# A hybrid attention layer on one core: difference product six segments later, four heads' sums in one bank, x's rows turned on TensorE

## The chip, the cores and the metric

One Trainium2 chip, one of its cores. The metric is the device time of one execution in microseconds (us), shorter is better; of several runs the median is given.

## The reference, cut to what matters

One layer over x of 2048 positions and 1024 channels, float32. The rows are RMS-normed and projected once; three causal mixers read the projection, each result is multiplied by a SiLU gate, and one output projection is added to x.

```python
h = rms_norm(x, norm_g)
proj = h @ w_in
# A: 8 heads of 64, softmax attention
sc = rms(q) . rms(k) / 8 + c[t] - c[s],   c = cumsum(log_sigmoid(ff + b_f))
fox = softmax(sc, s <= t) @ v
# B: 4 groups of 64
pool = (window_mean(px, w) - px) @ w_pool * scale,   w = 2, 4, 8, 16
# C: 4 heads of 64, stick-breaking
a[t, s] = sigmoid(z[t, s]) * prod over s < j < t of (1 - sigmoid(z[t, j]))
sb = a @ v
out = x + concat(fox * silu(fg), pool * silu(pg), sb * silu(sg)) @ w_out
```

The stick-breaking weights are differences of running products, so the kernel multiplies the running products by differences of neighbouring rows of v. It gets those differences from a small matrix product: this is the "difference product".

## The kernel before, in words

**Precision.** A value that a matmul reads is split into two fp16 halves, high and low (`pairs16`, L338: the high half on ScalarE at L340, the low one on VectorE at L341), and three products are summed (L318).

**Stages.** The 2048 positions are 16 blocks of 128, taken from the last to the first (i counts them, j = 15 - i is the place). There are five projections: Fox heads 0 to 3 ("a"), Fox heads 4 to 7 ("b"), stick-breaking ("s"), pooling ("p"), output ("o"). `units` lists them: 16 of a, 16 of b, 16 of s with the 16 of p between them, 16 of o. `projections` is one long generator over the units; a unit yields after each *segment*, 3 matmuls of 128x512, and has 16 segments (pooling 8). Each segment calls `tick`, which counts down the waiting list of `later(k, fn)`: fn is issued k segments later. At the start of a unit `need_x` makes the next unit's x.

**x.** In stage a, `make_x` (L362) loads 128 rows (xn, L345, on SP's queue), sums their squares (ScalarE L351), and `transpose_rows` (L370) splits them into ppx (L340, L341), transposes ppx into xTx by one DMA from SP's queue (L374, 2048 columns), and parks xTx in DRAM two segments later from ScalarE's queue (L380). Stages b, s and p load it from there. xTx has two buffers. The first three units (blocks 15, 14 and 13) are prepared in `opening`; block 15 is used there in another form, so it is made once more for its parked copy alone.

**Attention.** `plan` lists 48 rows of blocks, each with four heads. For one head `qk` computes the scores of a block against all later places in the list (PSUM tile sp, L403, with a mask product L405), and makes weights: for Fox VectorE adds the forget term and finds the maximum (L735), ScalarE takes exp (L745); for stick-breaking ScalarE takes the sigmoid (L874), POOL masks the diagonal (L876) and VectorE scans the product (L882). `split_t` (L415) splits the weights into pp (ScalarE L429, VectorE L432) and transposes pp into tt by DMA from SP's queue (L434). Three heads later (`DEPTH`) `pv` sums weights times values into a PSUM tile o (L445, L446; stick-breaking L902 to L904). The dictionary `LEADS` fixes how many segments of projection lie between these steps.

**What the change touches.** In Fox, a head's sums stand as 128 columns (high and low half of v) in a bank of their own; VectorE adds the two halves into om (L779) after each head, and after the fourth POOL multiplies om by the reciprocal sums (L758). In stick-breaking, three matmuls of 64 columns sum into 64 columns, and four heads share one tile (L902 to L904). `steps` (L813), called at the end of a stick-breaking unit, forms the difference product pd (L820) from the values vr that were split just before (L340, L341), and splits it into Vs and vo. The PSUM tiles pqk, pvg, pf, pd, o, pr and pp (pooling) come from one pool of four banks (tag "pj"); the scores have the other four.

**Order.** Each engine runs its instructions in a fixed order. It is chosen when the program is built: by priority and by an estimate of when each can start, so instructions of different steps can stand among each other.

Of the kernel before, what the change touches and what calls it, by code (L numbers as in the profile page):

```python
# [30 lines left out]
LB = 4  # L31
SPD = 6
KPD = 2
MXD = 0
GTD = 0
BAL = 1
# [70 lines left out]
M3 = 2  # L107
M4 = 2
HOOK2 = 4
X1 = 1  # L110
X0 = 2
PBK = 4
# [12 lines left out]
def hybrid(ctx: ExitStack, tc, xN, w_in, w_pT, w_out, ng, b_f, qg, kg, w_pool, p_scale, bands, out):  # L125
# [19 lines left out]
    def pick(pattern, k):  # L145
        return {"v": v, "g": g, "s": s}[pattern[k % len(pattern)]]
# [36 lines left out]
    g.affine_select(tri, ones, [[-1, P]], ALU.is_ge, 0.0, base=0, channel_multiplier=1)  # L183
    id16 = const.tile([P, P], BF16, name="id16")
    g.tensor_copy(id16, ident)
    zero = at.tile([P, P], BF16, name="zero", tag="oa")
    g.memset(zero, 0.0)
    cmask = const.tile([P, P], BF16, name="cmask")
# [181 lines left out]
    def transpose_rows(src, scale, tag, park=None):  # L370
        pp = at.tile([P, 2 * D], F16, name=f"pp{tag}", tag="pp", bufs=PB)
        pairs16(pp[:, 0:D], pp[:, D:2 * D], src, scale[:, 0:1], pick(XLO, park or 0))
        x = xp.tile([P, 2, KT, P], F16, name=f"xT{tag}", tag="xT", bufs=XB)
        sy.dma_start_transpose(x.rearrange("p a k t -> p (a k) t"), pp)  # L374
        if park is not None:
            keep_x(park, x)
        return x

    def keep_x(j, x):
        later(KPD, lambda: dq(QPARK).dma_start(xTd[j], x))  # L380
# [53 lines left out]
            sy.dma_start_transpose(tt[:, :2 * n * G // P, :], pp[:, :2 * n * G])  # L434
        return tt[:, o_ // P:(o_ + 2 * n) // P]

    def pv(o, h, parts, Vc):
        first = True
        for n_, (c0, c1_, tt) in enumerate(parts):
            nb = (c1_ - c0) // P  # L440
            for b in range(nb):
                jj = c0 // P + b
                vt = Vc[jj // 4][:, jj % 4, h, :]
                last = n_ == len(parts) - 1 and b == nb - 1
                t.matmul(o[:, 0:P], tt[:, b, :], vt, start=first, stop=False)  # L445
                t.matmul(o[:, 0:HD], tt[:, nb + b, :], vt[:, 0:HD], start=False, stop=last)  # L446
                first = False

    def heads(ap):
        return ap.rearrange("p (h d) -> p h d", h=NH)  # L450
# [42 lines left out]
    class Fox:  # L493
# [256 lines left out]
        def weighted(self, i, sums):  # L750

            la, n_ = sums
            if n_ == 2:
                v.tensor_tensor(la[:, 0], la[:, 0], la[:, 1], ALU.add)
            rl = sm.tile([P, NH], F32, name=f"rl{self.ph}_{i}", tag="rl")
            v.reciprocal(rl, la[:, 0])
            v.tensor_scalar(rl, rl, self.iv[:, 0:1], None, ALU.mult, ALU.bypass)
            pick(OMS, 0).tensor_tensor(heads(self.om), heads(self.om), rl.unsqueeze(2).broadcast_to([P, NH, HD]), ALU.mult)  # L758

        def pv(self, i, h, parts, rl):  # L760
            j = NT - 1 - i
            if h == 0:
                self.om = at.tile([P, 256], F32, name=f"om{self.ph}_{i}", tag="om")
            self.finish(self.om, h, parts, f"{self.ph}_{i}_{h}")
            if h == NH - 1:
                self.weighted(i, rl)
                c = self.col
                om = self.om

                def send():  # L770
                    dq(QMIX).dma_start(mix[j][:, c:c + 256], om)
                    mixed.add((self.ph, j))

                later(MXD, send)

        def finish(self, om, h, parts, tag):
            o = po.tile([P, 512], F32, name=f"o{tag}", tag=ot)
            pv(o, h, parts, self.Vc)
            v.tensor_reduce(om[:, h * HD:(h + 1) * HD], o[:, 0:P].rearrange("p (a d) -> p d a", a=2), AX.X, ALU.add)  # L779

# [3 lines left out]
    class Stick(Fox):  # L786
# [54 lines left out]
        def proj(self, i, x):  # L841
            w = self.w
            j = NT - 1 - i
            pqk = pj.tile([P, 512], F32, name=f"pqks_{i}", tag="pj")
            if i in IS:
                pvg = pj.tile([P, 512], F32, name=f"pvgs_{i}", tag="pj")
                yield from together([project(pqk, x, w, 0, 0, 512), project(pvg, x, w, 0, 512, 512)])
            else:
                yield from project(pqk, x, w, 0, 0, 512)
            qT = stacks(f"s_{i}", j, pqk[:, 0:256], pqk[:, 256:512], 1.0 / WS, self.Kc)  # L850
            if i not in IS:
                pvg = pj.tile([P, 512], F32, name=f"pvgs_{i}", tag="pj")
                yield from project(pvg, x, w, 0, 512, 512)
            vt = at.tile([P, NH, P], F16, name=f"vr_{i}", tag="fq", bufs=2)
            pairs16(vt[:, :, 0:HD], vt[:, :, HD:P], heads(pvg[:, 0:256]), 1.0 / WS)
            self.vr[i] = vt
            keep_gate("s", i, j, pvg[:, 256:512], w.iw, 768)
            self.steps(i, j)
            self.ctx[i] = qT

        def qk(self, i, h):
# [27 lines left out]
        def pv(self, i, h, parts, left):  # L889

            j = NT - 1 - i
            if h == 0:
                self.o = po.tile([P, 512], F32, name=f"os_{i}", tag=ot)
            o = self.o[:, h * HD:(h + 1) * HD]
            first = True
            for n_, (c0, c1_, tt) in enumerate(parts):
                nb = (c1_ - c0) // P
                for b in range(nb):
                    jj = c0 // P + b
                    vt = self.own[i][:, h] if jj == j else self.Vc[jj // 4][:, jj % 4, h, :]  # L900
                    last = n_ == len(parts) - 1 and b == nb - 1
                    t.matmul(o, tt[:, b, :], vt[:, 0:HD], start=first, stop=False)  # L902
                    t.matmul(o, tt[:, b, :], vt[:, HD:P], start=False, stop=False)
                    t.matmul(o, tt[:, nb + b, :], vt[:, 0:HD], start=False, stop=last)  # L904
                    first = False
            if h == NH - 1:
                om = at.tile([P, 256], F32, name=f"oms_{i}", tag="om")
                g.tensor_tensor(heads(om), heads(self.last), left.unsqueeze(2).broadcast_to([P, NH, HD]), ALU.mult)
                v.scalar_tensor_tensor(om, self.o[:, 0:256], self.io[:, 0:1], om, ALU.mult, ALU.add)
                self.own.pop(i)  # L910
                c = self.col

                def send():
                    dq(QMIX).dma_start(mix[j][:, c:c + 256], om)
                    mixed.add((self.ph, j))

                later(MXD, send)

# [200 lines left out]
    def projections():  # L1119
        for u, (n, i) in enumerate(units):  # L1120
            need_x(u + (2 if units[u + 2:u + 3] == [(4, 0)] and OA else LAH[n]))
            if i == 0 and n:
                phases[n].start()
            gen = phases[n].proj(i, xs.pop(u, None))
            yield from with_tail(gen) if (n, i) == (4, 0) else gen
            if i == NT - 1 and n < 3:
                with first(HLW):
                    load_weights((1, 2, 4)[n])
            if n == 2 and i == 1:
                load_weights(3)  # L1130
# [181 lines left out]
```

## Time and profile before

| | |
|---|---|
| median of 3 runs | 1382.42 us (1378.74 to 1386.62) |
| the profiled execution: its own time | 1382.85 us |
| its span, first to last instruction | 1381.1 us |
| mean granted TensorE clock | 0.943 of 2.4 GHz |
| TensorE busy | 1185.5 us (86%) |
| VectorE busy | 1006.6 us (73%) |
| ScalarE busy | 751.6 us (54%) |
| POOL busy | 304.6 us (22%) |

PE is TensorE's matmuls, PEld its weight loads, DVE is VectorE, ACT ScalarE, POOL GpSimd, SP the engine whose queue issues most DMAs. Times in the trace are us from the start of the span. "<-" behind a row names what ended the idle time before it. A busy TensorE is not one at its peak: durations of neighbouring matmuls overlap, so the pitch is read from the distance of their starts.

### The profile page before, as it was taken

What the parts mean: (1) busy time and instruction counts of PE and PEld (TensorE: products, weight loads), DVE (VectorE), ACT (ScalarE), POOL (GpSimd) and SP (SyncE); (2) the same over time, 40 slices, a digit from 0 to 9 for tenths busy, and PEclk for the clock granted to TensorE, in tenths of its full rate; (3) what the DMA queues carried; (4) which work ended last, traced back from release to release, by engine and by line L of the source; (5) the groups of instructions that cost most, each with busy time, mean ns of one, the idle gap of its engine ahead of it and who ended that gap; (6) DMA issues with size and microseconds to landing.
All of it is one profiled execution on the core that took longest, in us unless ns stands there. A gap on an engine that the chain in (4) does not pass through costs nothing.

```text
span 1381.1 us, 24952 instructions
## 1 busy us (share of the span) xinstructions
PE 1185.5 (86%) x9068; PEld 634.9 (46%) x9068; DVE 1006.6 (73%) x2165; ACT 751.6 (54%) x1429; POOL 304.6 (22%) x471
## 2 busy tenths in 40 slices
PE   7786978787887798998978888988996998779998
PEld 3343534344444355554545444444553554444443
DVE  5677868887887568789888765767785788956541
ACT  6456657666666457677667744545554565421210
POOL 0121221211011222112112252433321214313300
PEclk9888999898998899999999999999998999989999
DMA  6659999999999999999999987886898889999763
GB/s 220 175 127 209 215 207 187 233 205 204 245 212 196 232 196 244 202 192 198 178 243 187 206 190 165 180 180 147 179 178 158 157 202 269 217 273 293 203 179 92
DMA packets 617067, 275.25 MB, mean 199 GB/s; under 512 B 552560, under 2 KB 590832, under 8 KB 616944
## 3 DMA queue, kind: packets, MB, share of 16 engines
q1 hardware_dynamic: 605600, 239.93, 82.0%
q10 hardware_dynamic: 10832, 33.67, 7.9%
q8 instruction: 71, 1.16, 0.4%
q14 instruction: 52, 0.43, 0.1%
q0 software_dynamic: 512, 0.07, 0.0%
HBM read 102.60 MB, written 34.67 MB: 99 GB/s over the span
## 4 chain that ended last, share of the span: by engine, by line
PE 47%; DMA 21%; DVE 11%; issue 9%; ACT 6%; SPq 3%; POOL 2%; ACTq 0%; POOLq 0%; DVEq 0%
PE pr L318 8%; DMA tta<-ppa 5%; DMA ttb<-ppb 5%; PE pqkb L318 4%; PE pvgb L318 4%; PE pqks L318 4%; DMA xTx<-ppx 3%; DVE rrs L882 3%; PE pqka L318 3%; PE pvgs L318 3%; PE pvga L318 3%; PE pp L318 3%; PE spb L403 2%; PE spa L403 2%; PE sps L403 2%
## 5 line engine op out<-in xcount | busy, mean ns | idle before, releaser
L318 PE MATMUL pr<-wo,xTm 128*128 128x512 f16 x768 | 171.0, 384 | 8.4 <-DMA xTm<-ppm 5.7
L429 ACT CAST pps<-rrs 128x640 f16<-128x640 f32 (+7 forms) x96 | 76.1, 795 | 122.1 <-DVE rrs L882 106.5
L882 DVE TENSOR_TENSOR_SCAN rrs<-rrs 128x640 f32<-128x640 f32 (+7 forms) x64 | 104.3, 1636 | 50.3 <-POOL rrs L876 42.3
L318 PEld LDWEIGHTS <-xTm 128*128 128x128 f16 x768 | 75.4, 99 | 100.3 <-DMA xTm<-ppm 6.8
L318 PEld LDWEIGHTS <-xTs 128*128 128x128 f16 x768 | 74.1, 99 | 92.3 <-issue 10.8
L318 PEld LDWEIGHTS <-xTb 128*128 128x128 f16 x768 | 74.5, 101 | 85.0 <-issue 10.8
L745 ACT ACTIVATE La<-La,nma 128x640 f32<-128x640 f32 (+7 forms) x96 | 85.3, 889 | 49.4 <-DVE nma L739 44.5
L745 ACT ACTIVATE Lb<-Lb,nmb 128x640 f32<-128x640 f32 (+7 forms) x96 | 85.5, 891 | 48.3 <-DVE nmb L739 48.1
L318 PEld LDWEIGHTS <-xTx 128*128 128x128 f16 x720 | 70.4, 102 | 84.4 <-issue 16.4
L432 DVE TENSOR_TENSOR pps<-rrs,pps 128x640 f16<-128x640 f32 (+7 forms) x96 | 93.5, 988 | 16.4 <-ACT pps L429 16.0
L318 PE MATMUL pp<-auxp,xTp 128*128 128x512 f16 x384 | 97.8, 407 | 0.0
L318 PE MATMUL pqkb<-wb,xTb 128*128 128x512 f16 x384 | 96.6, 399 | 0.0
L432 DVE TENSOR_TENSOR ppb<-Lb,ppb 128x640 f16<-128x640 f32 (+7 forms) x96 | 87.8, 927 | 11.3 <-ACT ppb L429 11.2
L445 PE MATMUL oa<-Va,tta 128*128 128x128 f16 x544 | 62.5, 228 | 37.2 <-DMA tta<-ppa 30.1
L432 DVE TENSOR_TENSOR ppa<-La,ppa 128x640 f16<-128x640 f32 (+7 forms) x96 | 89.8, 954 | 5.5 <-ACT ppa L429 5.4
L318 PE MATMUL pqks<-ws,xTs 128*128 128x512 f16 x384 | 93.2, 388 | 0.4 <-ACT ws L276 0.4
L318 PE MATMUL pvgb<-wb,xTb 128*128 128x512 f16 x384 | 93.4, 386 | 0.0
L318 PE MATMUL pvgs<-ws,xTs 128*128 128x512 f16 x384 | 90.5, 379 | 1.7 <-DVE ym L1004 1.7
L874 ACT ACTIVATE rrs<-sps,nc 128x640 f32<-128x640 f32 (+7 forms) x96 | 79.9, 862 | 21.1 <-PE sps L403 11.6
L403 PE MATMUL spa<-Ka,qTa 128*128 128x512 f16 (+3 forms) x320 | 78.2, 357 | 13.4 <-DVE mma L735 12.0
L318 PE MATMUL pqka<-wa,xTx 128*128 128x512 f16 x336 | 87.1, 406 | 0.0
L445 PE MATMUL ob<-Vb,ttb 128*128 128x128 f16 x544 | 61.4, 224 | 28.7 <-DMA ttb<-ppb 28.2
(306 smaller groups left out, 2788.0 us busy)
## 6 DMA issues: line engine op xcount, KB each, us to landing
xn<-in_xN_dram SPq DMA_DIRECT2D x16, 512.0 KB, 5.4
xTd<-xTx ACTq DMA_DIRECT2D x16, 512.0 KB, 4.5
xTb<-xTd ACTq DMA_DIRECT2D x16, 512.0 KB, 4.4
xTs<-xTd ACTq DMA_DIRECT2D x16, 512.0 KB, 4.5
xTp<-xTd ACTq DMA_DIRECT2D x16, 512.0 KB, 3.9
go<-gat SPq DMA_DIRECT2D x16, 512.0 KB, 7.0
mt<-mix SPq DMA_DIRECT2D x16, 512.0 KB, 5.5
xr<-in_xN_dram SPq DMA_DIRECT2D x16, 512.0 KB, 4.5
```

The costliest lines, as they stand in the source:

```text
L318: t.matmul(psum, x[:, xa, kt, :], wt[:, wa, c0:c0 + n], start=(kt == 0 and i == 0), stop=(kt == KT - 1 and i == 2))
L403: t.matmul(sp[:, b - c0 + off:e - c0 + off], qT[:, a * NH + h, :], Kc[b // 512][:, h, b % 512:b % 512 + e - b], start=(a == 0), stop=(a == ...
L429: s.copy(hi, p32)
L432: lo_eng.tensor_tensor(lo, p32, hi, ALU.subtract)
L445: t.matmul(o[:, 0:P], tt[:, b, :], vt, start=first, stop=False)
L745: s.activation(ls[a], ls[a], AF.Exp, bias=nm[:, 0:1], accum_out=la[:, a, h:h + 1])
L874: s.activation(gg, sp, AF.Sigmoid, scale=self.nc2[:, 0:1])
L882: v.tensor_tensor_scan(gg, gg, gg, init, ALU.mult, ALU.bypass)
```

## The change

Three edits and two constants. `steps` is called six segments after the end of its unit and not at once. Fox's sums take stick-breaking's form: one function `pv` for both, three matmuls of 64 columns for a block, four heads in one tile o; L779 goes, and the multiplication by the reciprocals reads o itself, on VectorE. In stage a, `transpose_rows` splits as before, but the turning is issued eleven segments later: 16 transposes of 128x128 on TensorE against an fp16 identity, in two PSUM tiles of tag "pj", each copied into xT by ScalarE; xT is allocated only then. The output stage's transposes, and the two made in the opening for blocks 14 and 13, stay DMAs.

```diff
+TURN = 11
+STL = 6
+    idh = const.tile([P, P], F16, name="idh")
+    g.tensor_copy(idh, ident)
...
     def transpose_rows(src, scale, tag, park=None):
         pp = at.tile([P, 2 * D], F16, name=f"pp{tag}", tag="pp", bufs=PB)
         pairs16(pp[:, 0:D], pp[:, D:2 * D], src, scale[:, 0:1], pick(XLO, park or 0))
-        x = xp.tile([P, 2, KT, P], F16, name=f"xT{tag}", tag="xT", bufs=XB)
-        sy.dma_start_transpose(x.rearrange("p a k t -> p (a k) t"), pp)
-        if park is not None:
+        if park is None:
+            x = xp.tile([P, 2, KT, P], F16, name=f"xT{tag}", tag="xT", bufs=XB)
+            sy.dma_start_transpose(x.rearrange("p a k t -> p (a k) t"), pp)
+            return x
+        made_x = []
+
+        def turn():
+            x = xp.tile([P, 2, KT, P], F16, name=f"xT{tag}", tag="xT", bufs=XB)
+            for a in range(2):
+                pt = pj.tile([P, 1024], F16, name=f"pt{tag}_{a}", tag="pj")
+                for b in range(KT):
+                    t.transpose(pt[:, b * P:(b + 1) * P], pp[:, a * D + b * P:a * D + (b + 1) * P], idh)
+                s.copy(x[:, a], pt.rearrange("p (k t) -> p k t", k=KT))
+            made_x.append(x)
             keep_x(park, x)
-        return x
+
+        later(TURN, turn)
+        return made_x
...
-    def pv(o, h, parts, Vc):
+    def pv(o, parts, vt):
...
-                vt = Vc[jj // 4][:, jj % 4, h, :]
-                t.matmul(o[:, 0:P], tt[:, b, :], vt, start=first, stop=False)
-                t.matmul(o[:, 0:HD], tt[:, nb + b, :], vt[:, 0:HD], start=False, stop=last)
+                vh = vt(c0 // P + b)
+                t.matmul(o, tt[:, b, :], vh[:, 0:HD], start=first, stop=False)
+                t.matmul(o, tt[:, b, :], vh[:, HD:P], start=False, stop=False)
+                t.matmul(o, tt[:, nb + b, :], vh[:, 0:HD], start=False, stop=last)
...
-            pick(OMS, 0).tensor_tensor(heads(self.om), heads(self.om), rl.unsqueeze(2).broadcast_to([P, NH, HD]), ALU.mult)
+            om = at.tile([P, 256], F32, name=f"om{self.ph}_{i}", tag="om")
+            v.tensor_tensor(heads(om), heads(self.o[:, 0:256]), rl.unsqueeze(2).broadcast_to([P, NH, HD]), ALU.mult)
+            return om
...
             if h == 0:
-                self.om = at.tile([P, 256], F32, name=f"om{self.ph}_{i}", tag="om")
-            self.finish(self.om, h, parts, f"{self.ph}_{i}_{h}")
+                self.o = po.tile([P, 512], F32, name=f"o{self.ph}_{i}", tag=ot)
+            pv(self.o[:, h * HD:(h + 1) * HD], parts, lambda jj: self.Vc[jj // 4][:, jj % 4, h, :])
...
-        def finish(self, om, h, parts, tag):
-            o = po.tile([P, 512], F32, name=f"o{tag}", tag=ot)
-            pv(o, h, parts, self.Vc)
-            v.tensor_reduce(om[:, h * HD:(h + 1) * HD], o[:, 0:P].rearrange("p (a d) -> p d a", a=2), AX.X, ALU.add)
...
-            self.steps(i, j)
+            later(STL, lambda: self.steps(i, j))
...
+            if i not in self.own:
+                tick(1 << 30)
...
-            gen = phases[n].proj(i, xs.pop(u, None))
+            x = xs.pop(u, None)
+            if isinstance(x, list):
+                if not x:
+                    tick(1 << 30)
+                x = x[0]
+            gen = phases[n].proj(i, x)
```

A call `tick(1 << 30)` issues everything that still waits in the list at once.

## Rows read from the trace of the kernel before

**Rows 1.** The page: busy us of each engine, share of the span, instructions.
```profile
PE 1185.5 (86%) x9068; PEld 634.9 (46%) x9068; DVE 1006.6 (73%) x2165; ACT 751.6 (54%) x1429; POOL 304.6 (22%) x471
```

**Rows 2.** Busy us by stage; columns: stretch, length, PE, PEld, DVE, ACT, POOL, clock, DMA.
```profile
43.50:365.00 321.50, 259.15 (x2003) 142.27 (x1999) 246.63 (x785) 194.93 (x452) 61.85 (x87) 0.91 0.97 201
365.00:700.00 335.00, 296.49 (x2265) 163.25 (x2265) 263.47 (x654) 219.65 (x456) 59.75 (x83) 0.95 1.00 211
700.00:1150.00 450.00, 388.15 (x3336) 211.38 (x3337) 335.53 (x450) 252.12 (x408) 127.64 (x256) 0.95 0.86 182
```

**Rows 3.** TensorE's waits, 43.5 to 365 us; columns: total us, times, longest.
```profile
PE pf L327 <- DMA xTx<-ppx: 19.0, 6, 8.8
PE oa L445 <- DMA tta<-ppa: 17.6, 10, 6.3
...
PE pvga L318 <- DVE oma L779: 2.2, 1, 2.2
```

**Rows 4.** The chain that ended last, 43 to 365 us, by line (cut at its end).
```profile
by line: DMA tta<-ppa 15.0%; DMA xTx<-ppx 15.0%; PE pqka L318 14.8%; PE pvga L318 14.2%; PE spa L403 7.3%; issue 4.4%; PE oa L445 4.4%; DVE La L735 4.0%; DMA wrb<-in_w_in_dram 2.2%; DMA xTd<-xTx 2.2%; PE oa L446 2.0%; ACT La L745 1.3%; ACT 
```

**Rows 5.** TensorE's waits, 700 to 1150 us.
```profile
PE pd L820 <- ACT vr L340: 23.3, 6, 9.8
...
PE pd L820 <- DVE vr L341: 5.0, 2, 3.7
```

**Rows 6.** Timeline around the longest of these waits: start, length, instruction.
```profile
1063.37 0.37 PE L820 MATMUL pd<-vr,sel 128*128 128x256 f16 x1 [9.75 <-ACT vr L340]
1063.54 6.27 PE L318 MATMUL pp<-auxp,xTp 128*128 128x512 f16 x15
...
1061.99 1.04 ACT L429 CAST pps<-rrs 128x1024 f16<-128x1024 f32 x1 [6.16 <-DMA tts<-pps]
...
1074.52 2.16 DVE L882 TENSOR_TENSOR_SCAN rrs<-rrs 128x768 f32<-128x768 f32 x1 [2.15 <-POOL rrs L876]
```

**Rows 7.** Timeline of TensorE: four Fox pairs, from L446 to L446; 14 stick sums.
```profile
603.28 0.19 PE L446 MATMUL ob<-Vb,ttb 128*128 128x64 f16 x1
...
603.62 0.19 PE L446 MATMUL ob<-Vb,ttb 128*128 128x64 f16 x1
...
916.46 0.19 PE L903 MATMUL os<-Vs,tts 128*128 128x64 f16 x1
...
916.84 0.19 PE L904 MATMUL os<-Vs,tts 128*128 128x64 f16 x1
```

**Rows 8.** Groups of instructions: count, busy us, mean ns, idle us before them.
```profile
L779 DVE TENSOR_REDUCE oma<-oa 128x64 f32<-128x128 f32 x64 | 17.9, 282 | 25.2 <-PE oa L446 25.0
...
L779 DVE TENSOR_REDUCE omb<-ob 128x64 f32<-128x128 f32 x64 | 18.0, 283 | 19.2 <-PE ob L446 18.8 <-issue 0.3
...
L1004 DVE TENSOR_TENSOR ym<-po,auxp 128x256 f32<-128x256 f32 x16 | 6.6, 413 | 0.0
...
L758 POOL TENSOR_TENSOR omb<-omb,rlb 128x256 f32<-128x256 f32 x16 | 11.9, 744 | 70.0 <-issue 42.0 <-DVE nmb L739 21.1 <-DVE omb L779 6.6
```

**Rows 9.** Timeline: one row's first sum, and the last head's reduction.
```profile
253.66 0.22 PE L445 MATMUL oa<-Va,tta 128*128 128x128 f16 x1
...
281.89 0.29 DVE L779 TENSOR_REDUCE oma<-oa 128x64 f32<-128x128 f32 x1 [1.06 <-PE oa L446]
```

**Rows 10.** DMA issues: the transposes of x, median us from issue to landing.
```profile
xTx<-ppx SPq DMA_TRANSPOSE x16, 4.5
```

**Rows 11.** A group of ScalarE, 43.5 to 365 us: reading 128x512 out of PSUM.
```profile
L706 ACT ACTIVATE qna<-pqka 128x512 f32<-128x512 f32 x13 | 7.7, 589 | 8.7 <-PE pqka L318 8.3 <-DVE sta L341 0.4
```

**Rows 12.** Timeline: pvga's start and the next unit's split, first and last late one.
```profile
94.59 3.62 PE L318 MATMUL pvga<-wa,xTx 128*128 128x512 f16 x16
...
106.64 1.28 DVE L341 SCALAR_TENSOR_TENSOR ppx<-xn,r,ppx 128x1024 f16<-128x1024 f32 x1 [1.78 <-ACT ppx L340]
...
324.86 1.89 PE L318 MATMUL pvga<-wa,xTx 128*128 128x512 f16 x8
...
335.18 1.28 DVE L341 SCALAR_TENSOR_TENSOR ppx<-xn,r,ppx 128x1024 f16<-128x1024 f32 x1 [0.16 <-issue]
```

More of the change, by code (lines that the diff above doesn't have):

```diff
@@ L441, in pv @@
             for b in range(nb):
-                jj = c0 // P + b
-                vt = Vc[jj // 4][:, jj % 4, h, :]
+                vh = vt(c0 // P + b)
                 last = n_ == len(parts) - 1 and b == nb - 1
-                t.matmul(o[:, 0:P], tt[:, b, :], vt, start=first, stop=False)
-                t.matmul(o[:, 0:HD], tt[:, nb + b, :], vt[:, 0:HD], start=False, stop=last)
+                t.matmul(o, tt[:, b, :], vh[:, 0:HD], start=first, stop=False)
+                t.matmul(o, tt[:, b, :], vh[:, HD:P], start=False, stop=False)
+                t.matmul(o, tt[:, nb + b, :], vh[:, 0:HD], start=False, stop=last)
                 first = False
@@ L762, in pv @@
             if h == 0:
-                self.om = at.tile([P, 256], F32, name=f"om{self.ph}_{i}", tag="om")
-            self.finish(self.om, h, parts, f"{self.ph}_{i}_{h}")
+                self.o = po.tile([P, 512], F32, name=f"o{self.ph}_{i}", tag=ot)
+            pv(self.o[:, h * HD:(h + 1) * HD], parts, lambda jj: self.Vc[jj // 4][:, jj % 4, h, :])
             if h == NH - 1:
-                self.weighted(i, rl)
+                om = self.weighted(i, rl)
                 c = self.col
-                om = self.om
                 def send():
@@ L891, in pv @@
             j = NT - 1 - i
+            if i not in self.own:
+                tick(1 << 30)
             if h == 0:
                 self.o = po.tile([P, 512], F32, name=f"os_{i}", tag=ot)
[L894 to L905, printed above, removed]
+            pv(self.o[:, h * HD:(h + 1) * HD], parts, lambda jj: self.own[i][:, h] if jj == j else self.Vc[jj // 4][:, jj % 4, h, :])
             if h == NH - 1:
```

## The prediction

> **What bounds the kernel now.** I read the page first, for the whole span, then the busy time by stage, then the waits of TensorE stage by stage, and last the chain and single stretches of the timeline. TensorE is the busiest engine, 1185.5 us or 86% of the span [rows 1]. The stages differ, in the DMA too [rows 2]. From 43.5 to 365 us (first Fox group, where x is also made) TensorE is busy 259.2 of 321.5 us, so idle 62.3, at a mean granted clock of 0.91 (1 is 2.4 GHz, 0.5 is 1.2), with a DMA share of 0.97. The second Fox group (to 700) has 38.5 us of idle at a DMA share of 1.00; stick-breaking and pooling (to 1150) 61.9 us at 0.86. So time can come only from TensorE's idle stretches, and what fills them must not lengthen its work.
>
> What ended those stretches: in the first Fox stage x's transposed rows ended 19.0 us in 6 waits and the transposed probabilities 17.6 us in 10 [rows 3]. The chain says more than the idle time does: DMA of xTx holds 15.0% of the stage, some 48 us, as much as tta [rows 4]. In the stick stage the difference product (pd) waits for its own values: 23.3 us for ScalarE and 5.0 for VectorE, 28.3 in 8 waits [rows 5].
>
> **Part 1, the difference product six segments later.** Nothing is added or removed: at most six matmuls and two splits for each of 16 blocks move, no DMA moves, and they pass projection segments on TensorE and scans, casts and splits on ScalarE and VectorE. The longest wait shows what is behind them [rows 6]: the cast that ScalarE starts at 1061.99, just before vr, had waited 6.16 us for a DMA to free its buffer, and TensorE stands 9.75 us at the first pd with 15 ready matmuls of pp and the next scores behind it; the next scan starts only at 1074.52. By the code the stage has 384 segments (16 blocks of 16 and 16 of 8), in its 450 us [rows 2], so six are worth 7.0 us: that covers seven of the eight waits whole (0.9 to 4.5 us each) and 7.0 of the 9.75, 25.6 us in all. Late next are the second operands (Vs and vo), which must be there before the block's sum; three heads lie between. TensorE that runs ahead partly meets VectorE, busy 335.5 of 450 us [rows 2]. Bounds 0 and -28; I take **-15**, a little over half, because the largest stall is also one of the scan chain.
>
> **Part 2, four heads' sums in one bank.** Per block of probabilities a 128- and a 64-column matmul become three of 64. In the trace four pairs take 0.34 us, 85 ns a pair; of the stick sums, which have the new form already, the last of 14 starts 0.38 us after the first, 29 ns each, 88 for three [rows 7]. So the 1088 blocks of both Fox stages, one matmul more each, cost 3 us of TensorE. VectorE loses 128 reductions of 0.283 us (36 us) and gets 32 multiplications out of PSUM at 0.413 (pooling's row of that shape), 13 us; POOL loses 32 of 0.68 to 0.74 us [rows 8]. Not on TensorE's path by itself. But VectorE's queue also stands before the reductions for TensorE, 25.0 + 18.8 = 44 us [rows 8], with the score operations behind it; now it stands once a row instead of four times. I take **-5**; bounds -20 (half the waits) and +10, for the bank: it was held for four short times and is now held from the first head's sum to the last, 253.66 to about 282 us in one row of the trace [rows 9], out of four banks that pqka, pvga and pf also want.
>
> **Part 3, x's rows on TensorE.** Thirteen blocks are turned for their units (the fourth unit to the last), and one more is the first block, made a second time for its copy in DRAM: 14. It removes 14 DMA transposes, each 4.5 us to landing [rows 10], so some 63 us of a filled DMA, and their issues on SP's queue, whose later transposes move up. It adds 14 x 16 transposes of 128x128. No fp16 transpose is in the trace; the nearest row is a 128-column fp16 matmul, for which a pair less its 29 ns leaves 56 ns [rows 7]: 224 x 56 = 13 us, 14 at the stage's clock, bounds 12 and 25 (all at 1.2 GHz). A single such matmul's 0.22 us [rows 9] is the way through the array and overlaps the next one.
>
> It adds 28 copies of 128x1024 out of PSUM on ScalarE. A read of 128x512 takes 0.59 us [rows 11], so twice that at most, 1.0 to 1.18 us, 28 to 33 us on an engine busy 194.9 of 321.5 [rows 2]: covered, unless TensorE waits for them. The copy that parks x in DRAM moves too, on ScalarE's queue; who reads it comes a stage later.
>
> It also adds a wait. Before, x's split had until the unit's end; now TensorE stops at segment 11 if the split isn't done, with the rest of pvga, scores and sums behind it. I set each unit's segment 11 (the tenth pvga matmul) against the end of the next unit's split. In 7 of 13 units the split is later, 45 us in all; the first is late by 11 us (96.6 against 107.9), the last by 9 (327.4 against 336.5) [rows 12]. The other six have 1.8 to 4.8 us to spare. The instruction order on an engine is chosen when the program is built, by estimated readiness (pd matmuls stand inside other loops' sums), so some late turns will have been put behind other work, and where the split was late TensorE stood anyway, up to 8.8 us [rows 3]. I take a quarter, 11 us. Gains: the 19.0 of xTx, and half the 17.6 of tta because the DMA has 15% less to transpose (by the code 28672 of the 188416 columns that the first group transposes). -19 - 9 + 14 + 11 = **-3**; bounds -48 and +40, worked out below.
>
> **Sum.** -15 - 5 - 3 = -23 on the profiled execution's own 1382.85 us, 0.4 above the median of the runs, so 1359.4 from the median; I say **1359**.
>
> **Rivals.**
> *Turns wait for their splits (slower).* All 45 us come, the 19.0 go, 14 are added, tta brings nothing: +40 in the first Fox stage, with parts 1 and 2 as above +20: 1402. It decides once some 32 of the 45 us are stood out on TensorE (32 - 19 + 14 - 20 = +7). For it: ScalarE and VectorE are in order, and the splits lie behind exps and casts. Against: VectorE loses 23 us of work, and the order is chosen anew.
>
> *The DMA was the bound there.* Its share is 0.97 in the stage [rows 2]; 63 us less of it can bring no more than TensorE's idle time, 62.3, less the turns' 14: -48, the bound. Three quarters of that, -36, with parts 1 and 2 make -56: 1326. For it: xTx's 15% of the chain [rows 4]. Against: only 36.6 of the idle us are put down to transposes.
>
> *Banks run out (no change).* One wait for a bank stands in the stage, 2.2 us before pvga [rows 3]. If each of 13 turns meets a full set once for each of its two tiles at half that, 13 x 2.2 = 29 us cancel the -23: 1389, inside the half per cent. Perfetto Trace Analysis of the Trainium skill, Matmuls, speaks for this: independent groups should rotate through banks so that emptying one overlaps filling the next, and the change does the opposite. The trace agrees only so far: the stick sums share a bank already, and bank waits are few there.
>
> *Transposes don't overlap (slower).* If each turn's matmul waits for the one before, 224 x 0.22 us [rows 9] are 49 instead of 14: 1394. Against it: in every row here matmuls of this size overlap. The Trainium skill, TensorE: Matmul & The Clock Gate, Part 4, gives 275 ns for a 128x128 transpose in a kernel; by that figure, an estimate, 224 take 62 us and the sum is 1407. No transpose of this type is in the trace to agree or not.
>
> **How the numbers follow.** Forecast 0.45 (1345 to 1374, its own range), DMA-bound 0.20, banks 0.14, late turns 0.17, no overlap 0.04. About half a per cent, 7 us, is what a measurement can tell from no change: faster 0.65, same 0.14, slower 0.21. The range leaves out the far end of the DMA case and over half of the late turns: 1325 to 1397.
>
> **What would show it.** Right: pd's waits under 5 us; L779 gone, VectorE some 23 us less; no wait of pf for xTx by DMA; SP with 14 fewer transposes; the first stage shorter by less than 15 us, the stick stage by 10 to 20. Wrong: TensorE's waits before the turns over 20 us, or waits for pj banks (before pvga, pf, the turns) over 10; or the first stage shorter by over 25, when the DMA was the bound. If the stick stage is not shorter though pd no longer waits, VectorE's scans bound it.

## The result, and the profile after

Measured beside the kernel before on one chip, five runs each: 1370.2 us (1366.56 to 1372.67) against 1386.62 (1378.74 to 1387.77), a ratio of 0.9899 with a 95% interval from 0.987 to 0.9929 (the two medians alone would give 0.988). The change makes the kernel 1.0% faster; the prediction was 1359 us, 1.7% faster. The profiled execution took 1372.67 us, its span is 1371.0 at a mean granted clock of 0.945.

Busy time of the engines, from the page of the kernel after, which answers to [rows 1]:

```profile
PE 1202.0 (88%) x10380; PEld 653.9 (48%) x10380; DVE 996.3 (73%) x2069; ACT 776.5 (57%) x1457; POOL 274.0 (20%) x440
```

TensorE has 16.5 us more work, ScalarE 24.9 more, VectorE 10.3 less. So the gain is idle time of TensorE, and the question is in which stage. Busy time by stage, columns as in [rows 2], each kernel cut at its own last pvga, last pvgb and last pvgs matmul. The kernel before:

```profile
43.50:361.70 318.20, 256.45 (x1969) 140.52 (x1966) 245.28 (x783) 192.69 (x450) 61.85 (x87) 0.91 0.96 199
361.70:695.00 333.30, 295.23 (x2274) 162.93 (x2272) 259.81 (x649) 217.10 (x449) 59.75 (x83) 0.95 1.00 211
695.00:1139.40 444.40, 385.88 (x3343) 210.88 (x3341) 330.58 (x447) 250.20 (x408) 124.47 (x251) 0.95 0.86 181
1139.40:1381.10 241.70, 215.71 (x1355) 104.42 (x1353) 143.50 (x206) 62.74 (x68) 55.94 (x34) 0.96 0.82 218
```

The kernel after:

```profile
43.50:349.40 305.90, 268.87 (x2604) 155.22 (x2602) 241.12 (x754) 220.37 (x484) 54.33 (x75) 0.94 0.86 189
349.40:691.50 342.10, 294.57 (x2740) 164.37 (x2741) 251.33 (x594) 212.28 (x445) 51.18 (x67) 0.94 0.99 199
691.50:1130.20 438.70, 391.04 (x3570) 214.91 (x3568) 329.48 (x443) 252.47 (x408) 113.75 (x247) 0.95 0.90 185
1130.20:1371.00 240.80, 216.12 (x1355) 103.72 (x1352) 148.65 (x206) 62.82 (x68) 51.85 (x34) 0.96 0.84 219
```

Read the lengths down the two: the first Fox stage lost 12.3 us, the second **gave 8.8 back**, the stick stage lost 5.7 and the output 0.9: 10.1 in all. In the first stage TensorE's idle time (length less PE) fell from 61.8 to 37.0 while its work grew by 12.4, and the DMA share fell from 0.96 to 0.86. In the second TensorE's work is the same and its idle time grew from 38.1 to 47.5.

TensorE's waits over the whole span of the kernel after (total us, times, longest), which answer to [rows 3, 5]:

```profile
PE ob L463 <- DMA ttb<-ppb: 43.7, 21, 8.2
PE oa L463 <- DMA tta<-ppa: 32.5, 20, 4.9
PE pr L322 <- DMA xTm<-ppm: 13.8, 3, 5.7
...
PE ptx L388 <- ACT ppx L344: 6.5, 2, 3.3
PE sps L420 <- POOL qTs L487: 6.4, 2, 4.1
PE pqks L322 <- DVE vo L345: 5.8, 2, 3.9
...
PE pd L835 <- DVE vr L345: 2.4, 1, 2.4
...
PE ptx L388 <- DVE ppx L345: 1.4, 2, 0.7
...
PE pd L835 <- ACT vr L344: 0.2, 1, 0.2
```

The same view of the kernel before, for three of the lines that grew:

```profile
PE oa L445 <- DMA tta<-ppa: 30.1, 18, 6.3
PE ob L445 <- DMA ttb<-ppb: 28.2, 12, 7.7
...
PE pr L318 <- DMA xTm<-ppm: 5.7, 3, 2.9
```

The two waits that the change went for are gone: pd's 28.3 us are 2.6, and pf no longer waits for x by DMA (19.0). In their place stand 15.5 us more before the second Fox stage's sums (ob), and 8.1 more before the output product (pr), for the transposes of its own input. Two lines are new, both in the stick stage: the scores (sps) wait 6.4 us for POOL, which copies qTs, and the projection pqks waits 5.8 for VectorE. pqks doesn't read vo; it takes a bank of the pool in which pd stands, and the split into vo is what reads pd last. Neither wait is in the kernel before. So in the stick stage, where pd's waits ended, TensorE's idle time fell only from 58.5 to 47.7 us.

### The profile page after: what moved, and what is told of

The parts are those of the page before. It is cut to its first block, busy times and chain, and to the rows that moved or that the text cites. A ratio compares the mean times of both kernels' runs of the same rounds, so it can differ in the third digit from the quotient of the medians.

```text
span 1371.0 us, 27421 instructions
## 1 busy us (share of the span) xinstructions
PE 1202.0 (88%) x10380; PEld 653.9 (48%) x10380; DVE 996.3 (73%) x2069; ACT 776.5 (57%) x1457; POOL 274.0 (20%) x440
## 3 DMA queue, kind: packets, MB, share of 16 engines
q8 instruction: 81, 1.33, 0.4%
## 4 chain that ended last, share of the span: by engine, by line
PE 50%; DMA 20%; issue 10%; DVE 10%; ACT 6%; POOL 2%; SPq 1%; ACTq 0%; POOLq 0%; DVEq 0%
PE pr L322 11%; DMA ttb<-ppb 8%; DMA tta<-ppa 7%; DVE rrs L897 5%; PE pqkb L322 5%; PE pvgb L322 5%; PE pvga L322 4%; PE pqka L322 3%; PE spb L420 3%; PE pqks L322 3%; PE pvgs L322 2%; PE spa L420 2%; PE pp L322 2%; PE sps L420 1%; DMA xTm<-ppm 1%
## 5 line engine op out<-in xcount | busy, mean ns | idle before, releaser
L322 PE MATMUL pr<-wo,xTm 128*128 128x512 f16 x768 | 173.1, 387 | 15.5 <-DMA xTm<-ppm 13.8
L446 ACT CAST pps<-rrs 128x640 f16<-128x640 f32 (+7 forms) x96 | 76.1, 795 | 115.2 <-DVE rrs L897 97.9
L897 DVE TENSOR_TENSOR_SCAN rrs<-rrs 128x640 f32<-128x640 f32 (+7 forms) x64 | 105.3, 1651 | 40.8 <-POOL rrs L891 30.9
L322 PE MATMUL pqks<-ws,xTs 128*128 128x512 f16 x384 | 98.8, 403 | 7.1 <-DVE vo L345 5.8
L449 DVE TENSOR_TENSOR pps<-rrs,pps 128x640 f16<-128x640 f32 (+7 forms) x96 | 88.9, 937 | 20.0 <-ACT pps L446 19.5
L463 PE MATMUL ob<-Vb,ttb 128*128 128x64 f16 x544 | 62.7, 199 | 44.5 <-DMA ttb<-ppb 43.7
L449 DVE TENSOR_TENSOR ppa<-La,ppa 128x640 f16<-128x640 f32 (+7 forms) x96 | 89.2, 947 | 10.6 <-ACT ppa L446 10.2
L322 PE MATMUL pvgs<-ws,xTs 128*128 128x512 f16 x384 | 94.2, 388 | 1.6 <-DVE ym L1010 1.6
L754 DVE CUSTOM_DVE_ANT_0 Lb<-spb,negcb,c 128x640 f32<-128x640 f32 (+7 forms) x64 | 60.2, 945 | 47.7 <-PE spb L420 28.9
L322 PE MATMUL pqkb<-wb,xTb 128*128 128x512 f16 x384 | 92.6, 387 | 0.7 <-DVE wb L281 0.7
L322 PE MATMUL pp<-auxp,xTp 128*128 128x512 f16 x384 | 92.2, 387 | 0.7 <-DVE vo L345 0.6
L463 PE MATMUL oa<-Va,tta 128*128 128x64 f16 x544 | 60.2, 199 | 32.7 <-DMA tta<-ppa 32.5
```

The source lines that it names most:

```text
L322: t.matmul(psum, x[:, xa, kt, :], wt[:, wa, c0:c0 + n], start=(kt == 0 and i == 0), stop=(kt == KT - 1 and i == 2))
L446: s.copy(hi, p32)
L449: lo_eng.tensor_tensor(lo, p32, hi, ALU.subtract)
L463: t.matmul(o, tt[:, b, :], vh[:, 0:HD], start=first, stop=False)
L754: v.tensor_tensor_reduce(lt, sp, negc[:, h, c0:c1_], c1[:, 0:1], 4 * NEG if a == 0 else mm[:, a - 1:a], ALU.add, ALU.max, mm[:, a:a + 1])
L897: v.tensor_tensor_scan(gg, gg, gg, init, ALU.mult, ALU.bypass)
```

## The experiments

Each is made from the kernel before or after by the edit shown; a ratio is to the kernel before on the same chip, with its 95% interval.

| kernel | parts | median us | ratio | interval |
|---|---|---|---|---|
| e1 | 1 | 1360.86 | 0.9867 | 0.9835 to 0.9898 |
| e2 | 2 | 1382.36 | 1.0016 | 0.9989 to 1.0043 |
| e3 | 3 | 1373.26 | 0.9945 | 0.9917 to 0.9974 |
| e4 | 2 and 3 | 1374.85 | 0.9965 | 0.9935 to 0.9996 |
| e5 | 1 and 3 | 1362.66 | 0.988 | 0.9843 to 0.9916 |
| e6 | 1 and 2 | 1378.44 | 1.0004 | 0.9977 to 1.0032 |
| after | 1, 2 and 3 | 1370.2 | 0.9899 | 0.987 to 0.9929 |

### One part at a time

**e1, the difference product alone** (part 1):

```diff
+STL = 6
...
-            self.steps(i, j)
+            later(STL, lambda: self.steps(i, j))
...
+            if i not in self.own:
+                tick(1 << 30)
```

> Part 1 alone (difference product six segments later, the rest as before). Theory A (the stall of pd is real time on the chain of the stick stage): pd's waits fall from 28 us to under 5, both Fox stages stay as they are within 2 us, and the whole is 5 to 12 us shorter. Rival B (the wait only moves to the next late thing, scans or casts): pd's waits fall the same, but the whole is within 3 us of before.

Measured 1360.86 us: 1.3% faster, some 18 us, more than the whole change. TensorE's waits of this kernel:

```profile
PE ob L461 <- DMA ttb<-ppb: 32.8, 16, 9.8
PE oa L461 <- DMA tta<-ppa: 28.5, 18, 5.7
PE pf L329 <- DMA xTx<-ppx: 18.2, 6, 8.9
...
PE pr L320 <- DMA xTm<-ppm: 10.6, 2, 5.7
...
PE pd L836 <- DVE vr L343: 3.2, 3, 2.3
```

Against the kernel before pd's waits fell from 28.3 to 3.2, and pr's wait for xTm rose from 5.7 to 10.6. TensorE's idle time over the whole span (the span less PE) fell by 24.9 us, from 195.6 to 170.7, and its work grew by 4.0. So theory A had the direction, with less than came: the wait was on the path that sets the end. Its condition on the Fox stages missed: they are 315.3 and 340.4 us here, 318.2 and 333.3 before, and the stick stage alone is 21.4 shorter. One thing that is late next is the output stage's own DMA transposes. That is a pattern, not one profile: all seven kernels with part 1 show 10.3 to 13.8 us of it, all seven without (the kernel before among them) 2.7 to 6.7. The two new waits of the stick stage are here as well, 5.2 us for qTs and 4.7 for vo; each of them stands in most kernels with part 1, and in no kernel without it over 0.3.

**e2, the shared bank alone** (part 2):

```diff
-            self.finish(self.om, h, parts, f"{self.ph}_{i}_{h}")
+            pv(self.o[:, h * HD:(h + 1) * HD], parts, lambda jj: self.Vc[jj // 4][:, jj % 4, h, :])
...
+            v.tensor_tensor(heads(om), heads(self.o[:, 0:256]), rl.unsqueeze(2).broadcast_to([P, NH, HD]), ALU.mult)
```

> Part 2 alone (four heads' sums in one bank). Theory C (the second Fox stage, 333 us before and 342 after the whole change, is longer because the bank is held and the sums are read later): this kernel shows it too, its second Fox stage is 5 to 10 us longer and the whole 3 to 10 us slower. Theory D (that stage is filled by the transposes of the probabilities and only gave back what part 3 won in the stage before): this kernel's stages are within 3 us of before or shorter, the whole 0 to 6 us faster.

Measured 1382.36 us, no change that can be told from none, though VectorE lost 96 instructions. Its waits:

```profile
PE ob L448 <- DMA ttb<-ppb: 42.0, 20, 7.8
PE oa L448 <- DMA tta<-ppa: 34.6, 17, 6.4
PE pd L820 <- ACT vr L342: 20.7, 5, 7.3
```

No wait for a bank of the pool "pj" stands among the larger ones. What grew most, by 18.3 us, is the wait for the transposed probabilities. Neither theory came: the first Fox stage is 6.1 us longer and the second 18.6, more than theory C has, yet the whole is not slower by what could be told.

**e3, the turns alone** (part 3), `transpose_rows` as in the change, nothing else:

> Part 3 alone (x's rows turned on TensorE). Theory D: projections of the first Fox stage end 10 to 14 us earlier than before (at about 349 us), the second stage is 6 to 10 us longer, and the whole is only 2 to 5 us faster. Theory C: the 10 to 14 us stay, and the whole is 9 to 14 us faster. In both, no wait for xTx by DMA is left from the fourth unit on, and SP issues 14 transposes fewer.

Measured 1373.26 us, 0.6% faster, some 8 us, between what the two theories expected (its runs go from 1363 to 1385; the profiled one was the fastest, so its stage lengths stand at the short end).

### Pairs of parts

**e4**, the change with one constant back:

```diff
-STL = 6
+STL = 0
```

> Parts 2 and 3 without part 1. If the parts add up, the time is that of before less the gains of the two single kernels; by theory A it lacks the 5 to 12 us that part 1 brings, so 1374 to 1382 us; by rival B it is as fast as the whole change within 3 us.

Measured 1374.85 us, 0.9965, inside theory A's range. The two parts alone sum to 1.0016 - 0.0055 = 0.9961: these two add.

**e5**, the change with Fox's sums as before (a bank for each head, L779 and POOL's multiplication back):

> Parts 1 and 3 without part 2. Seen so far: ratio 0.987 for part 1 alone, 1.002 for part 2, 0.994 for part 3, 0.990 for all three, which is less than the sum; and in the one profile of each, TensorE's waits for transposed probabilities (tta and ttb) are 58 to 62 us without part 2 and 76 us with it. Theory E (part 2 is what costs, because sums that need no new bank are put on TensorE ahead of their transposes): waits for tta and ttb 57 to 64 us, ratio 0.978 to 0.984. Theory F (parts 1 and 3 take the same time out, so that they don't add): ratio 0.987 to 0.992.

Measured 1362.66 us, 0.988, theory F's side; the waits for tta and ttb, 67.1 us, lie above what theory E names. Parts 1 and 3 do not add: their sum would be 0.9867 - 0.0055 = 0.981, below the interval. With part 1 alone in, part 3 brings nothing that could be told.

**e6**, the change with `transpose_rows` as before:

> Parts 1 and 2 without part 3. Theory E: waits for tta and ttb 72 to 80 us, ratio 0.988 to 0.994, slower than part 1 alone by 1 to 7 us. Theory F: as fast as part 1 alone within 2 us, 0.985 to 0.989.

Measured 1378.44 us, 1.0004. It misses what either theory expected: part 1's 1.3% is gone when part 2 is in and x is still turned by DMA. Against e1 the two Fox stages are 19 us longer, and what lies behind them is 3 us shorter.

### What the shared bank costs

**e7**: part 2's three matmuls, but a bank for each head as before, and a copy in place of the reduction:

```diff
+            o = po.tile([P, 512], F32, name=f"o{tag}", tag=ot)
+            pv(o[:, 0:HD], parts, lambda jj: self.Vc[jj // 4][:, jj % 4, h, :])
+            v.tensor_copy(om[:, h * HD:(h + 1) * HD], o[:, 0:HD])
```

> Of part 2 only the form: three matmuls of 64 columns, but each head in a bank of its own, copied out by VectorE as the reduction was, and POOL multiplies as before. Theory E (the shared bank sets the order): waits for tta and ttb back at 56 to 66 us. Theory G (the form with three matmuls does it, for instance by the time that they take): 72 to 80 us as with part 2. Time for both within 0.5% of before.

**e9**: the reverse, four heads in one bank but the old form, a 128- and a 64-column matmul, with one reduction for the four heads and POOL's multiplication:

```diff
+            pv2(self.o[:, h * P:(h + 1) * P], h, parts, self.Vc)
...
+                v.tensor_reduce(self.om, self.o.rearrange("p (h a d) -> p h d a", h=NH, a=2), AX.X, ALU.add)
```

> Part 2 turned round: four heads share a bank, but each keeps the pair of a 128- and a 64-column matmul (four times 128 columns fill the bank), and one VectorE reduction of the whole row replaces four; POOL multiplies as before. Theory G (the three-matmul form is what costs, seen as 77 us of waits for tta and ttb with own banks too): waits for tta and ttb 56 to 68 us, ratio 0.992 to 1.002. Theory J (the sharing, or any new order of the build, costs as much): waits over 70 us, ratio 1.003 to 1.013.

Measured 1398.02 us for e7 (1.0133, 1.0097 to 1.017) and 1401.19 for e9 (1.0127, 1.0083 to 1.0171). The waits of e7:

```profile
PE ob L448 <- DMA ttb<-ppb: 40.1, 20, 7.9
PE oa L448 <- DMA tta<-ppa: 37.4, 17, 6.9
```

and of e9:

```profile
PE ob L461 <- DMA ttb<-ppb: 39.8, 20, 7.2
PE oa L461 <- DMA tta<-ppa: 25.7, 14, 6.2
```

Both halves of part 2, each with its own reading of the sums, are slower than part 2 whole. For the waits e7 sides with theory G (77.5 us with banks of their own, so the form and not the sharing goes with them), but its time lies far outside what was expected. For the time e9 sides with theory J, but with waits of 65.5, hardly more than the 58.3 of before. So these waits do not account for the time, and neither the sharing nor the form alone is the cost. The two are slow in different ways. The page of e7:

```profile
PE 1199.5 (86%) x10156; PEld 642.5 (46%) x10156; DVE 1003.3 (72%) x2165; ACT 751.2 (54%) x1429; POOL 306.3 (22%) x471
```

TensorE is busy 14.0 us longer than before [rows 1], and its span of 1395.1 us is 14.0 longer: by this page all that the profiled execution lost is TensorE's own work, none of it more standing. The mean granted clock is 0.935, against 0.943 before. e9's span is 15.2 us longer, of which 12.3 are idle time of TensorE and 2.9 work.

One reading does part the kernels by the sharing: VectorE's wait for the scores of the second Fox group. Groups of VectorE in the kernel before (columns as in [rows 8]):

```profile
L735 DVE CUSTOM_DVE_ANT_0 Lb<-spb,negcb,c 128x640 f32<-128x640 f32 (+7 forms) x64 | 59.9, 944 | 19.5 <-PE spb L403 12.8 <-DMA negcb<-cd 6.4
```

in the kernel after, with the reading of the sums:

```profile
L778 DVE TENSOR_TENSOR oma<-oa,rla 128x256 f32<-128x256 f32 x16 | 6.7, 421 | 10.8 <-PE oa L465 10.7
L778 DVE TENSOR_TENSOR omb<-ob,rlb 128x256 f32<-128x256 f32 x16 | 6.7, 420 | 5.6 <-PE ob L465 5.6
...
L754 DVE CUSTOM_DVE_ANT_0 Lb<-spb,negcb,c 128x640 f32<-128x640 f32 (+7 forms) x64 | 60.2, 945 | 47.7 <-PE spb L420 28.9 <-PE spb L422 14.1 <-DMA negcb<-cd 4.4
```

and in e7:

```profile
L739 DVE CUSTOM_DVE_ANT_0 Lb<-spb,negcb,c 128x640 f32<-128x640 f32 (+7 forms) x64 | 60.2, 943 | 16.2 <-PE spb L405 11.7 <-DMA negcb<-cd 4.2 <-PE spb L407 0.2
```

VectorE stood 44 us before the reductions [rows 8]; before the multiplications it stands 16.3. But at the scores this row's wait for TensorE grew from 12.8 to 43.0. Over all fourteen kernels it is 30.9 to 43.0 in the seven where four heads share a bank (e2, e4, e6, e9, e10, e11, after) and 11.9 to 20.0 in the seven where they don't. **The wait moved, it was not removed.** The reductions, four times a row, were where VectorE stood for TensorE; without them it runs ahead and stands for the same engine at the next scores. In all seven kernels with the shared bank VectorE also reads the sums once a row and not four times, so no run tells whether the bank or the single reading does it.

**e10**: e9's sums with parts 1 and 3.

> The same bank with pairs, together with parts 1 and 3 (0.988 without any part 2; the whole change 0.990). Theory G: no worse than parts 1 and 3, ratio 0.981 to 0.989. Theory J: 0.990 to 1.000.

Measured 1368.84 us, 0.9922 (0.9887 to 0.9957), theory J's side: beside the other two parts the pair form gives the time of the whole change, though alone (e9) it is 1.3% slower than before.

### Is it the DMA?

**e8**: e3, and on SP's queue at the place of each removed transpose a plain copy of the same 512 KB into spare DRAM:

```diff
+    junkd = [dr.tile([P, 2 * D], F16, name=f"junkd{j}", tag=f"junkd{j}") for j in range(NT)]
...
+        sy.dma_start(junkd[park], pp)
         made_x = []
```

> Part 3 alone, and where the DMA transpose of x was issued, SP now issues a plain copy of the split rows (512 KB) into a spare DRAM tile that nobody reads, 14 in all: the DMA engines get about the load back, x doesn't wait for it. Theory H (part 3 gains because x arrives without the DMA's delay): the gain stays, ratio 0.991 to 0.998, TensorE's waits for tta in the first Fox stage as in part 3 alone within 4 us. Theory I (it gains because the transposes of the probabilities get a freer DMA): the gain goes, ratio 0.998 to 1.004, and waits for tta rise by over 6 us.

Measured 1366.77 us, 0.991 (0.9885 to 0.9935). The stage's row, the DMA's group and the waits:

```profile
43.50:352.30 308.80, 266.71 (x2152) 152.54 (x2151) 242.84 (x774) 214.95 (x474) 68.23 (x87) 0.93 0.95 203
```

```profile
junkd<-ppx SPq DMA_DIRECT2D x14, 512.0 KB, 3.3
```

```profile
PE oa L478 <- DMA tta<-ppa: 34.6, 23, 4.6
PE ob L478 <- DMA ttb<-ppb: 22.3, 16, 2.7
```

The copies fill the DMA again, share 0.95 against 0.91 in e3 and 0.96 before, and the kernel is no slower than e3. That is theory H: the gain is not the relief of the DMA's share, for it stays when most of the relief is taken away. The sign on tta is at its edge: in the first Fox stage the wait is 14.9 us, 10.9 in e3. A plain copy is not a transpose, so e8 does not shut out that fewer transposes are what helps. Against that, the waits for tta in that stage are 10.9 to 22.7 us in the seven kernels with turns and 14.2 to 17.6 in the seven without.

### Is it the order, and is there a better one?

The order is chosen anew for every build, so the ratios could be luck of it. **e11** is the whole change one segment off in both constants:

```diff
-TURN = 11
+TURN = 12
...
-STL = 6
+STL = 5
```

> The whole change with its two delays moved by one segment (difference product five later, turning twelve later): the same work, nearly the same places, but the build deals the order of instructions anew. Theory K (a new order alone moves the time by 0.5 to 1.5%, which is why the parts don't add): the ratio differs from the whole change's 0.990 by over 0.004. Theory L (the order is steady, the parts act on each other): 0.987 to 0.993.

Measured 1371.61 us, 0.9926 (0.9894 to 0.9958). **e12** is e1 with a longer delay:

```diff
-STL = 6
+STL = 8
```

> Part 1 alone with eight segments in place of six (0.987 with six). pd's waits are gone either way, under 5 us. Theory L: ratio 0.983 to 0.991. Theory K: 0.992 to 1.005, the gain of part 1 alone being half order and half the wait.

Measured 1358.37 us (1354.51 to 1365.84), 0.984 (0.9808 to 0.9871). In e11 pd waits again, 14.2 us, as five segments cover less than six. Both are theory L's: neighbouring orders give neighbouring times, for the whole and for part 1 alone. No neighbour of e6, e7 or e9 was built, so for those three an unlucky order is not shut out. e12 has the lowest ratio of the study, though its interval overlaps e1's: it beats the kernel before by 1.6%, and its interval ends below 0.9899, the ratio of the whole change. Of its waits:

```profile
PE pf L329 <- DMA xTx<-ppx: 18.6, 6, 8.0
...
PE pr L320 <- DMA xTm<-ppm: 10.3, 3, 4.8
...
PE pd L836 <- DVE vr L343: 2.1, 1, 2.1
```

## Why the prediction was right, and which terms were not

**The total.** Forecast -23 us of 1382; measured 1.0%, some 14. The time lies in the range and the likeliest case came. The three parts measured alone sum to -1.33 + 0.16 - 0.55 = -1.72%, 24 us: almost the sum on record. That agreement is luck: the single terms are off by 3, 7 and 5 us, and the errors cancel. **The step that failed is the addition itself.** "-15 - 5 - 3 = -23" takes each part's gain as free of the others, and together they give 14. What is lost goes with part 1, by the table: with part 2 beside it 1.2% of the gain is lost (e6), with part 3 0.7% (e5), while parts 2 and 3 add (e4).

**Part 1: -15 on record, -18 alone.** The reasoning held: pd's waits are under the 5 us named, and the eighth wait ended too. "Late next" named the second operands, and vo is indeed late, but it is the next projection that stands for it, through pd's bank (5.8 us), and not the block's sum. Not foreseen were the scores' wait for qTs (6.4 us) and, a stage later, the transposes of the output's input (5 to 8 us more before pr). The stick stage is 5.7 us shorter in the whole change, and not the 10 to 20 named as a sign of being right. Beside other parts it is worth 0.1% (with part 2) to 0.7%: a mean over its four differences of 0.69%, 9.5 us. In the whole change the last stick sum ends at 1231.5 us, 15.6 earlier than before, and the span 10.1: 5.5 us are lost behind it, where pr waits 8.1 longer.

**Part 2: -5 on record, +2 alone and a mean of +0.48%, +7.** Three of its four differences are 0.16 to 0.20%, which no run tells from nothing; the fourth, e6 against e1, is 1.37%. The instructions came as costed: L779 is gone, 32 multiplications of 0.42 us stand in its place. The failed step is "half the waits", 20 us of gain as its bound: VectorE's wait before the sums did fall by 28 us, and the wait for the scores took its place, 30 us in one row. VectorE's busy time fell by 10 us, not 23. Part of that is that other operations ran longer in this execution (the low halves of the output's splits have a mean of 1.48 us, 1.28 before, 3 us in all); but part 2 takes off only 12 to 16 us in any of its four differences, so the 23 were too many from the start. Why was not found.

**Part 3: -3 on record, -8 alone and a mean of -0.50%, -7.** Here the terms were of the right kind and one was far off.

- *The turns' work.* Forecast 224 transposes at 56 ns, 14 us. The timeline of the kernel after, merged rows of eight transposes, two halves at full clock and two from a late turn:

```profile
130.56 0.61 PE L388 MATMUL ptx<-idh,ppx 128*128 128x128 f16 x8
...
132.03 0.61 PE L388 MATMUL ptx<-idh,ppx 128*128 128x128 f16 x8
...
223.17 0.62 PE L388 MATMUL ptx<-idh,ppx 128*128 128x128 f16 x8 [3.12 <-ACT ppx L344]
224.49 1.03 PE L388 MATMUL ptx<-idh,ppx 128*128 128x128 f16 x8 [0.70 <-DVE ppx L345]
```

  0.61 us less one transpose's 0.22 leaves seven pitches of 56 ns. The late turn's second half, after TensorE had stood 3.12 and 0.70 us, has a pitch of 116 ns ((1.03 - 0.22) / 7, 107 by the starts) at a granted clock of 0.54, that is near 1.2 GHz. The groups of TensorE, then of ScalarE, show the duration and the copies:

```profile
L388 PE MATMUL ptx<-idh,ppx 128*128 128x128 f16 x224 | 17.6, 226 | 8.5 <-ACT ppx L344 6.5 <-DVE ppx L345 1.4 <-ACT xTx L389 0.4
```

```profile
L389 ACT COPY xTx<-ptx 128x1024 f16<-128x1024 f16 x28 | 27.9, 1007 | 10.5 <-PE ptx L388 9.4 <-DMA xTd<-xTx 0.7 <-PE pqkv L322 0.4
```

  28 copies are 27.9 us, the low end of 28 to 33, and covered but for 2.0 us that TensorE waits for them.
- *Late turns: 11 us on record, 8 measured* (6.5, 1.4 and 0.4 before ptx), nearly all in two turns, where the rival feared 45 in seven. Most splits run earlier than feared: the first late one, which ended at 107.9 us before, ends at 94.0, and its turn starts at 96.5. The two that were late (turns at 223.2 and 322.8 us) cost 4 us each.
- *tta: -9 on record, nothing measured.* Before the first group's sums TensorE waits 18.4 us in the stage of the kernel after, against 17.6, although the DMA share fell by 0.10. e8 shows the same from the other side: a filled DMA does not cost the gain.
- *Terms that were not on record.* With what was measured the terms give -19 + 14 + 8 = +3, and the part brought -7. TensorE's waits from 43.5 us to the last pvga show ten more. In the kernel before, beside those of [rows 3], among others:

```profile
PE spa L403 <- DVE mma L735: 8.0, 6, 4.5
PE pbb L252 <- DVE mma L735: 4.6, 1, 4.6
PE oa L445 <- DVE mma L735: 3.3, 1, 3.3
```

  and in the kernel after:

```profile
PE spa L420 <- DVE mma L754: 3.8, 6, 1.2
...
PE pbb L256 <- DVE mma L754: 1.6, 1, 1.6
```

  All waits of that stage but those for xTx, tta and before ptx sum to 24.9 us in the kernel before, and to 9.9 after, 14.9 in e5 and 15.7 in e8, two other kernels with turns. So TensorE stands 9 to 15 us less for its other operands, VectorE's above all: while it stood for x before, and the work behind x came late, VectorE came late with it. That last is a reading of the order, and no run was made for it alone. The second is the clock. The stage's row in e5:

```profile
43.50:348.00 304.50, 265.93 (x2194) 152.84 (x2192) 244.94 (x785) 219.09 (x480) 60.83 (x87) 0.95 0.92 188
```

  The mean granted clock of the first Fox stage is 0.89 to 0.91 in the seven kernels without turns and 0.92 to 0.97 in the seven with them. In e5 the stage has 225 matmul records more than before, as many as the 224 turns and one, forecast at 14 us of work, but TensorE's busy time grew by 9.5. That the higher clock gave back the rest fits, but no run parts it from the shorter waits.
- *Stage length.* "Shorter by less than 15 us" held, 12.3. That the second stage would give 8.8 back was not foreseen. A part is only work that moves over the boundary: in all seven kernels with turns the two Fox stages together are 2 to 13 us shorter than in the kernel before, whatever the first one gained (24.3 in e3, 5.1 in e4).

**The rivals.** *Late turns* fell by the 8.3 us above, a quarter of the 32 from which it decides. *The DMA was the bound* fell by e8, and by its own sign: the first stage is 12.3 us shorter, not over 25. *Transposes don't overlap* fell by the 56 ns. The Trainium skill, TensorE: Matmul & The Clock Gate, Part 4, gives 275 ns for one in a kernel. The trace differs: a transpose lasts 226 ns, near that figure, but the next starts after 56, so the figure is no pitch. *Banks run out* is not borne out for the shared bank: part 2 did take a part of the gain, but the waits before pvga, pf and the turns that would show a lack of banks are not there. The largest wait for a bank of that pool in the kernel after is the 5.8 us before pqks, which part 1 brings. The Trainium skill, Perfetto Trace Analysis, Matmuls, wants independent groups in rotating banks. Here e7, which keeps a bank for each head, is 1.3% slower than before: the sums' rotating banks alone do not make this kernel faster.

**What stays open.** Why part 2 costs time is not settled. It is not longer waits for banks of "pj", and not the sharing alone nor the form alone (e7, e9). TensorE's longer work, forecast at 3 us, is not shut out for the small differences: by the pages its busy time is 12.3, 5.6 and 6.0 us longer where part 2 is added to the kernel before, to e3 and to e5. But where part 2 cost most, e6 against e1, it is 0.7 us longer and the span 16.3: there TensorE stands more. That e6 is an unlucky order of the build was not tested. The stages don't tell it either: in e2 the two Fox stages are 24.7 us longer, but all that stands behind them is 20.8 shorter. That VectorE waits at the scores instead is shown; that this is the cost is only argued, since e7 has no such wait and is slow too. Why parts 1 and 3 don't add (e5) was not found either.

## What to carry to other kernels

Time the parts of a bundled edit alone and in pairs before keeping it: here one constant (the difference product eight segments later) is worth 1.6%, and the whole bundle 1.0%. A matmul that waits for operands made just before it is cheap to move back by a few segments, where the wait lies on the very path that sets the end; then look for what is late next, in the same stage and one stage on. Taking away an instruction at which an engine stood for another can move the standing to the next meeting of the two, as it did here, so count it as a gain only if nothing behind it waits for the same engine.

## What the runs showed of the hardware

- Back to back, fp16 transposes of 128x128 on TensorE follow each other every 56 ns, like the 128-column matmuls of the Fox pairs (85 less 29 ns, [rows 7]), and run at the full granted clock (1.00 in the first half of the turn at 223 us); 16 of them and two copies of 1.0 us replace a DMA that took 4.5 us to land.
- ScalarE copies 128x1024 fp16 out of PSUM in 1.007 us, 0.17 us less than twice the 0.589 us of its fp32 activation of 128x512 [rows 11].
- Fourteen plain copies of 512 KB, landing in 3.3 us each, cost nothing that could be told in a stage whose DMA share they raised from 0.91 to 0.95 (e8 at 0.991, e3 at 0.9945): a share near 1 did not mean here that the DMA set the time.
